# Hybrid attention and expert block: attention heads issued in three steps, and a split first product

## The chip, the cores and the metric

One core of a Trainium2 chip runs one program. The metric is the device time of one execution in microseconds (us). Each kernel is run several times and the median counts. One further execution is taken with the profiler on, and all rows below come from that one.

## What is computed

The reference is one decoder layer on 256 tokens of width 2048, in float32:

```
h   = RMSNorm(x)
z   = h @ w_in          # q, k, v of the window attention; q, kv, rope key of the latent attention; two gates
y_a = window attention, 16 heads of 64, 4 key heads, sinks and ALiBi   @ w_a_proj
y_b = latent attention, 8 heads of 128 + 64 rope, values of 128        @ w_b_proj
x   = x + (sigmoid(g_a) * y_a + sigmoid(g_b) * y_b) @ w_o
x   = x + PEER(RMSNorm(x))      # 8 heads, 16 of 16384 experts each
out = RMSNorm(x)
```

## The kernel before

**Numbers and weights.** Every float32 weight or activation is kept as a high part that TensorE reads at full rate and a low part, the remainder. `feed_hi` (L100) loads one megabyte of weights, 16 tiles of 128 x 128, into a ring of three buffers (SP's queue), ScalarE (ACT) makes the high part `whi` (L108) and VectorE (DVE) the low part `wlo` (L112), both in rings of two. `tblock` (L142) is one projection block of 128 output columns: for each of `nk` depth blocks a matmul of the high weight with the activation's high and low part side by side (L145, 512 columns), then for each one of the low weight with the activation's high part (L149, 256 columns). `tproj` (L343) is such a block over all 16 depth blocks, followed by `both` (L151: one copy on ACT, one addition on DVE) and a scaling (L346). `split` (L138) is the pair of an ACT copy and a DVE subtraction that makes an activation's two parts.

**Order.** Up to the expert part (`manual_schedule`, L920) the order of instructions on each engine is made by the framework's planner: it steps through an estimated time line and gives each engine the earliest program line whose operands it believes ready by then. Each engine works its list in order. Program order is thus a priority, and an engine waits when the real operands are later than the planner thought.

**Around the change.** The queries' eight blocks (`qT`, L448) come first. Then `gates(sga)` (L566) makes 16 blocks for the first gate, and after each one `work.pull(2.2)` (L569) lets the generator `swa` (L482) go on. `Work.pull` (L54) keeps an account: the budget is added, each yielded cost is taken off, and the generator runs while the account is positive. `swa` yields 2.0 after each head and 0.4 after each pair of heads. One head: four logit matmuls (`lg`, L498 and L499); softmax on DVE and ACT in `row_max`, `exps` (L452) and the first lines of `probs_T` (L460); three transposes of the normalised row `lt` (`tp`, L467); a split into `pT` (L513); six products with the values (`ot`, in `pv`, L476). Two heads share an `ot`, whose split (L516) fills one of the eight parts of `ya`.

`branch` (L573) then makes 16 blocks of half depth from `ya` and the first gate, with `work.pull(0.9)` for the latent heads' generator `mla` (L519): ten logit matmuls a head, and the operands of a head (`qns`, `kns`, `qrs`, `vs`) split in `prepare`, called for head h + 1 behind head h's products. `gates(sgb)` runs 16 blocks for the second gate, with the rest of `mla` beside them.

Later, the attention's output projection (L617) ends with a chain per block: `both`, the residual (L621), the gain (L631) and the split into `xc` (L632). The first of the 16 blocks of the expert queries (`tblock(ps, KO, xc)`, L781) needs all 16 parts of this `xc`, the last made last. Its transposes `x1t` (L611) are those of the residual rows. Behind it stands a matmul with ones (L786) for the norm.

Of the kernel before, what the change touches and what calls it, by code (L numbers as in the profile page):

```python
# [8 lines left out]
F32 = mybir.dt.float32  # L9
# [56 lines left out]
def block(tc, a, out):  # L66
# [72 lines left out]
        act.activation(hi, src, AF.Copy)  # L139
        vec.tensor_tensor(lo, src, hi.bitcast(F32), op=OP.subtract)  # L140

    def tblock(ps, nk, act_c, between=None):  # L142
        ws = take(nk)
        for k, (wh, wl) in enumerate(ws):
            pe.matmul(ps, wh, act_c[:, k].rearrange("p a t -> p (a t)"), start=k == 0, stop=False)  # L145
        if between:
            between()
        for k, (wh, wl) in enumerate(ws):
            pe.matmul(ps[:, :T], wl, act_c[:, k, 0], start=False, stop=k == nk - 1)  # L149

    def both(pl, ps):  # L151
        t = pl.tile([P, T], F32, name="both", bufs=2)
# [190 lines left out]
    def tproj(dst, scale=1.0):  # L343
        ps = acc_tile()
        tblock(ps, KO, xc)
        vec.scalar_tensor_tensor(dst, both(x0p, ps), scale, r1, op0=OP.mult, op1=OP.mult)  # L346
# [98 lines left out]
    for h in range(NH_B):  # L445
        uproj(knT[:, h], 2, ckvT)
    tmpp.close()
    for b in range(8):  # L448
        tproj(qT[:, b], 0.125)


    def exps(lt, m):  # L452
        nm = wk.tile([P, 2], F32, name="nm")
# [3 lines left out]
        act.activation(lt[:, 128:384], lt[:, 128:384], AF.Exp, bias=nm[:, 1:2], accum_out=ssm[:, 1:2])  # L457
        return nm, ssm

    def probs_T(lt, ssm):  # L460
        rec = wk.tile([P, 2], F32, name="rec")
        vec.reciprocal(rec, ssm)
        vec.tensor_scalar(lt[:, 0:128], lt[:, 0:128], rec[:, 0:1], None, op0=OP.mult)
        vec.tensor_scalar(lt[:, 128:384], lt[:, 128:384], rec[:, 1:2], None, op0=OP.mult)
        tp = tp_tile()
        for k in range(3):
            pe.transpose(tp[:, k * P:(k + 1) * P], lt[:, k * P:(k + 1) * P], ident)  # L467
        return tp

    def row_max(lt):  # L470
        m = wk.tile([P, 2], F32, name="mx")
# [4 lines left out]
    def pv(ot, vh, vl, pT, first, last):  # L476
        for c, o, ks in ((0, slice(0, 256), slice(0, 256)), (1, slice(128, 256), slice(256, 384))):
            pe.matmul(ot[:, o], vh[:, c], pT[:, 0, ks], start=first and c == 0, stop=False)
            pe.matmul(ot[:, o], vh[:, c], pT[:, 1, ks], start=False, stop=False)
            pe.matmul(ot[:, o], vl[:, c], pT[:, 0, ks], start=False, stop=last and c == 1)  # L480

    def swa(yc):  # L482
        def prepare(b):
            qs = wk.tile([P, 2, T], F32R, name="qs", bufs=1)
            stacked(qs, qT[:, b])
            return qs

        qs = prepare(0)
        for b in range(8):
            kp, i = b // 4, b % 4  # L490
            ot = ps_att.tile([P, 512], F32, name="ot", bufs=1)
            for half in range(2):
                g = 2 * kp + half
                h = g * 4 + i
                lg = ps_att.tile([P, 512], F32, name="lg", bufs=1)
                for q, ks, o in ((slice(0, 128), slice(0, 128), slice(0, 128)),
                                 (slice(128, 256), slice(0, 256), slice(128, 384))):
                    pe.matmul(lg[:, o], qs[:, half, q], kk[:, g, ks], start=True, stop=False)  # L498
                    pe.matmul(lg[:, o], qs[:, half, q], kl[:, g, ks], start=False, stop=True)  # L499
                if half and b < 7:  # L500
                    qs = prepare(b + 1)
                lt = wk.tile([P, 384], F32, name="lt", bufs=2)
                vec.scalar_tensor_tensor(lt, dist, -(2.0 ** (-8.0 * (h + 1) / NH_A)), lg[:, 0:384],
                                         op0=OP.mult, op1=OP.add)
                m = row_max(lt)
                vec.tensor_scalar(m, m, sink[:, h:h + 1], None, op0=OP.max)
                nm, ssm = exps(lt, m)
                e = wk.tile([P, 2], F32, name="esink")
                act.activation(e, nm, AF.Exp, bias=sink[:, h:h + 1])
                vec.tensor_tensor(ssm, ssm, e, op=OP.add)  # L510
                tp = probs_T(lt, ssm)
                pT = wk.tile([P, 2, 384], F32R, name="pTs", bufs=1)
                split(pT[:, 0], pT[:, 1], tp[:, 0:384])  # L513
                pv(ot, vap[:, 0, :, g], vap[:, 1, :, g], pT, half == 0, half == 1)
                yield 2.0
            split(yc[:, b, 0], yc[:, b, 1], ot[:, 0:256])  # L516
            yield 0.4

    def mla(yc):  # L519
        scale = 192.0 ** -0.5  # L520

        def prepare(h):
            if h % 2 == 0:
                qr[:] = [mw.tile([P, 2, T], F32R, name="qrs")]
                stacked(qr[0], qrT[:, h // 2])
            qn, kn = (mw.tile([P, 2, T], F32R, name=n) for n in ("qns", "kns"))
            split(qn[:, 0], qn[:, 1], qnT[:, h])
            split(kn[:, 0], kn[:, 1], knT[:, h])
            vs = mw.tile([P, 2, 2, P], F32R, name="vs")
            split(vs[:, 0], vs[:, 1], vb[:, :, h * P:(h + 1) * P])  # L530
            return qr[0], qn, kn, vs

        qr = []
        ops = prepare(0)
        for h in range(NH_B):
            half = h % 2
            qrs, qn, kn, vs = ops
            lg = ps_att.tile([P, 512], F32, name="lg", bufs=1)
            for q, ks, o in ((slice(0, 128), slice(0, 128), slice(0, 128)),
                             (slice(128, 256), slice(0, 256), slice(128, 384))):  # L540
                pe.matmul(lg[:, o], qn[:, 0, q], kn[:, 0, ks], start=True, stop=False)
                pe.matmul(lg[:, o], qn[:, 0, q], kn[:, 1, ks], start=False, stop=False)
                pe.matmul(lg[:, o], qn[:, 1, q], kn[:, 0, ks], start=False, stop=False)
                pe.matmul(lg[:, o], qrs[:, half, q], krT[:, 0, ks], start=False, stop=False)
                pe.matmul(lg[:, o], qrs[:, half, q], krT[:, 1, ks], start=False, stop=True)
            lt = wk.tile([P, 384], F32, name="lt", bufs=2)
            vec.scalar_tensor_tensor(lt, lg[:, 0:384], scale, cmask, op0=OP.mult, op1=OP.add)
            m = row_max(lt)
            nm, ssm = exps(lt, m)
            tp = probs_T(lt, ssm)  # L550
            pT = wk.tile([P, 2, 384], F32R, name="pTs", bufs=1)
            split(pT[:, 0], pT[:, 1], tp[:, 0:384])
            ot = ps_att.tile([P, 512], F32, name="ot", bufs=1)
            pv(ot, vs[:, 0], vs[:, 1], pT, True, True)
            if h + 1 < NH_B:
                ops = prepare(h + 1)
            yield 2.0
            split(yc[:, h, 0], yc[:, h, 1], ot[:, 0:256])
            yield 0.4

# [3 lines left out]
    def gates(sg):  # L566
        for b in range(KO):
            tproj(sg[:, b])
            work.pull(2.2)  # L569
        for q in range(4):  # L570
            act.activation(sg[:, 4 * q:4 * q + 4], sg[:, 4 * q:4 * q + 4], AF.Sigmoid)

# [5 lines left out]
    ya = yp.tile([P, 8, 2, T], F32R, name="ya", tag="y0")  # L578
    sga = yp.tile([P, KO, T], F32, name="sga")
    work.add(swa(ya))  # L580
    gates(sga)
    work.drain()
    swp.close()
# [3 lines left out]
    work.add(mla(yb))  # L587
    for b in range(KO):
        branch(ya, sga, x0p, b)
        work.pull(0.9)  # L590
    sgb = yp.tile([P, KO, T], F32, name="sgb", tag="y0")
    gates(sgb)
    work.drain()
# [184 lines left out]
    behind = None  # L778
    for hp in range(16):
        ps = acc_tile()  # L780
        tblock(ps, KO, xc)  # L781
        if hp:
            work.pull(1.2)
        if hp == 0:
# [399 lines left out]
```

## Time and profile before

| what | us |
|---|---|
| median of 3 runs | 1921.58 (1920.23 to 1923.5) |
| profiled execution, its own time | 1917.56 |
| span of that execution | 1915.8 |
| mean granted clock of TensorE over the span | 0.994 |
| queries' blocks, from the first one to the first logits | 108.1 to 158.1 |
| first gate's blocks with the window attention | 158.1 to 271.7 |
| branch blocks and second gate's blocks with the latent attention | 271.7 to 433.3 |
| first block of the expert queries, start to its norm's matmul | 572.0 to 581.2 |

In the trace an engine's line is its busy time; for TensorE, PE is matmuls and PEld the weight loads that run beside them. Matmuls are pipelined: a row's duration is longer than the distance to the next row's start, so prices of matmuls are read from starts. "idle before" in brackets is the time for which the engine stood before that instruction, and the instruction that ended it. The granted clock is given in parts of full speed, 1.0 for 2.4 GHz and 0.5 for 1.2 GHz, averaged over a stretch.

### The profile page before, as it was taken

The numbers are of one execution on the slowest core, as the hardware profiler recorded it, in microseconds if no ns is written. First come the engines' busy times: TensorE is split into PE (matmuls) and PEld (weight loads), VectorE is DVE, ScalarE is ACT, GpSimd is POOL, SyncE is SP. The second block draws the span as 40 slices with busy tenths as digits, with TensorE's granted clock in tenths as the row PEclk, the third lists the DMA queues.
The fourth block names the chain that finished last, engine by engine and source line by source line (L and its number), as shares of the span: only waits on it lengthen the run. The fifth ranks groups of instructions, "written<-read, shape, count | busy, mean of one in ns | idle before, by whom it ended". The sixth has DMA issues, their size and how long they took to land.

```text
span 1915.8 us, 28101 instructions
## 1 busy us (share of the span) xinstructions
PE 1871.1 (98%) x10874; PEld 1678.5 (88%) x10874; DVE 1594.7 (83%) x2277; ACT 1142.5 (60%) x1756; POOL 360.1 (19%) x192
## 2 busy tenths in 40 slices
PE   8999999999999999999999999999999999999996
PEld 6888888888888899999999999988888888887885
DVE  5767879658778889989799999899888888878887
ACT  7645666545555554555899999864444444444444
POOL 0000000000000000516243433333322222233210
PEclk9999999999999999999999999999999999999998
DMA  7554434455555566666889888879999999999983
GB/s 285 187 189 154 141 123 153 147 184 189 202 198 181 176 206 234 220 238 241 309 337 352 345 339 344 343 303 373 366 394 373 382 386 380 378 397 378 393 337 127
DMA packets 77910, 526.16 MB, mean 275 GB/s; under 512 B 9168, under 2 KB 11472, under 8 KB 15568
## 3 DMA queue, kind: packets, MB, share of 16 engines
q1 hardware_dynamic: 59344, 390.14, 56.4%
q0 software_dynamic: 18432, 134.23, 17.2%
q8 instruction: 85, 1.39, 0.3%
q14 instruction: 49, 0.40, 0.1%
HBM read 520.14 MB, written 4.19 MB: 274 GB/s over the span
## 4 chain that ended last, share of the span: by engine, by line
PE 64%; issue 13%; DVE 8%; POOL 7%; DMA 4%; ACT 4%; SPq 0%; POOLq 0%; DVEq 0%; ACTq 0%
PE acc L145 15%; PE o L1008 11%; PE acc L149 8%; POOL urow L803 7%; PE acc L927 6%; PE o L1025 5%; PE o L1026 5%; PE o L1027 5%; PE acc L956 4%; DVE wlo L112 3%; DMA raw<-v 3%; ACT whi L108 2%; PE acc L165 1%; PE acc L166 1%; PE acc L164 1%
## 5 line engine op out<-in xcount | busy, mean ns | idle before, releaser
L112 DVE TENSOR_TENSOR wlo<-raw,whi 128x2048 fp32r<-128x2048 f32 (+2 forms) x363 | 827.1, 2279 | 215.9 <-ACT whi L108 203.5
L108 ACT ACTIVATE whi<-raw 128x2048 fp32r<-128x2048 f32 (+2 forms) x363 | 688.6, 1897 | 435.1 <-DMA raw<-v 179.7
L927 PE MATMUL acc<-hc,whi 128*128 128x384 f32 x2048 | 383.0, 339 | 0.2 <-ACT whi L108 0.2
L927 PEld LDWEIGHTS acc<-hc,whi 128*128 128x128 f32 x2048 | 353.2, 189 | 0.4 <-ACT whi L108 0.4
L956 PE MATMUL acc<-hc,wlo 128*128 128x192 f32 x2048 | 251.2, 274 | 4.9 <-DVE wlo L112 4.9
L1008 PE MATMUL o<-wlo,wc 128*128 128x512 f32 x1020 | 252.2, 389 | 1.0 <-DVE wlo L112 1.0
L956 PEld LDWEIGHTS acc<-hc,wlo 128*128 128x128 f32 x2048 | 243.4, 192 | 6.0 <-DVE wlo L112 5.9
L145 PE MATMUL acc<-xc,whi 128*128 128x512 f32 x928 | 231.1, 395 | 1.5 <-DVE xc L140 1.5
L1008 PEld LDWEIGHTS o<-wlo,wc 128*128 128x128 f32 x1020 | 191.3, 188 | 41.4 <-DVE wlo L112 1.7
L803 POOL DMA_INDIRECT urow<-u_rows,iv x64 | 167.1, 2611 | 314.0 <-DVE urow L827 311.0
L1025 PE MATMUL o<-whi,wc 128*128 128x512 f32 x504 | 196.6, 390 | 3.6 <-ACT whi L108 1.8
L145 PEld LDWEIGHTS acc<-xc,whi 128*128 128x128 f32 x928 | 168.4, 188 | 32.5 <-DVE xc L140 1.7
L1026 PE MATMUL o<-whi,wc 128*128 128x512 f32 x504 | 196.1, 389 | 0.0
L1027 PE MATMUL o<-whi,wc 128*128 128x512 f32 x504 | 196.1, 389 | 0.0
L803 POOL DMA_INDIRECT vrow<-v_rows,iv x64 | 126.2, 1972 | 333.2 <-DVE h_nat L840 299.4
L827 DVE SCALAR_TENSOR_TENSOR urow<-urow,h_nat 128x2048 f32<-128x2048 f32 x64 | 146.2, 2284 | 21.4 <-DMA urow<-u_rows,iv 21.3
L696 POOL TENSOR_TENSOR cand<-tv 128x256 f32<-128x256 f32 x16 | 14.0, 891 | 739.4 <-DVE tv L689 642.4
L840 DVE SCALAR_TENSOR_TENSOR h_nat<-vrow,gg,h_nat 128x2048 f32<-128x2048 f32 x63 | 147.8, 2346 | 0.0
L877 ACT ACTIVATE ge<-acc 128x192 f32<-128x192 f32 x128 | 41.3, 323 | 151.5 <-PE acc L956 146.7
L149 PE MATMUL acc<-xc,wlo 128*128 128x256 f32 x928 | 126.1, 286 | 0.0
L149 PEld LDWEIGHTS acc<-xc,wlo 128*128 128x128 f32 x928 | 121.4, 193 | 4.3
L1025 PEld LDWEIGHTS o<-whi,wc 128*128 128x128 f32 x504 | 94.6, 188 | 24.7 <-ACT whi L108 3.1
(329 smaller groups left out, 2255.1 us busy)
## 6 DMA issues: line engine op xcount, KB each, us to landing
raw<-u SPq DMA_DIRECT2D x128, 1024.0 KB, 5.0
raw<-v SPq DMA_DIRECT2D x128, 1024.0 KB, 8.7
raw<-w_ga SPq DMA_DIRECT2D x16, 1024.0 KB, 4.9
raw<-w_gb SPq DMA_DIRECT2D x16, 1024.0 KB, 5.0
raw<-w_o SPq DMA_DIRECT2D x16, 1024.0 KB, 5.0
raw<-w_pq SPq DMA_DIRECT2D x16, 1024.0 KB, 5.0
raw<-w_q SPq DMA_DIRECT2D x8, 1024.0 KB, 4.9
raw<-w_a SPq DMA_DIRECT2D x8, 1024.0 KB, 4.8
```

The costliest lines, as they stand in the source:

```text
L108: act.activation(hi, raw, AF.Copy)
L112: vec.tensor_tensor(lo, raw, hi.bitcast(F32), op=OP.subtract)
L145: pe.matmul(ps, wh, act_c[:, k].rearrange("p a t -> p (a t)"), start=k == 0, stop=False)
L149: pe.matmul(ps[:, :T], wl, act_c[:, k, 0], start=False, stop=k == nk - 1)
L803: pool.indirect_dma_start(out=dst, out_offset=None, in_=table, in_offset=bass.IndirectOffsetOnAxis(ap=idx, axis=0))
L840: later(vec.scalar_tensor_tensor(h_nat, r, gg[:, i:i + 1], h_nat, op0=OP.mult, op1=OP.add))
L927: pe.matmul(ps[:, :2 * TD], wh, hc[:, k].rearrange("p a t -> p (a t)"), start=k == 0, stop=False)
L956: pe.matmul(ps[:, :TD], wl, hc[:, k, 0], start=False, stop=k == KO - 1)
L1008: pe.matmul(O[c][i], st_, v[:, i * 512:(i + 1) * 512], start=first and k == 0, stop=last and k == len(ss) - 1)
L1025: pe.matmul(O[0][i], S[0], vh[:, d], start=n == 0, stop=False)
L1026: pe.matmul(O[0][i], S[1], vh[:, d], start=False, stop=False)
L1027: pe.matmul(O[1][i], S[2], vh[:, d], start=n == 0, stop=False)
```

## The change

Three things are changed. `tblock` can put the last `late` depth blocks behind the others, high and low parts of the first ones first; the first block of the expert queries uses this with two. `probs_T` loses the normalisation (now `normalised`) and gains the split into `pT`. A new generator, `staged`, runs the heads in steps: each step does the products (`back`) of the head two before, the transposes and their split (`probs_T`) of the head before, and the operands, logits and softmax (`front`) of its own head, and yields 2.0. `swa` and `mla` are written as `front` and `back`. The generator of the window attention is now started before the queries' blocks, which pull 1.7 each from the second on; `gates` pulls 1.7 in place of 2.2, the branch blocks 0.8 in place of 0.9.

```diff
@@ -139,14 +139,16 @@
         act.activation(hi, src, AF.Copy)
         vec.tensor_tensor(lo, src, hi.bitcast(F32), op=OP.subtract)
 
-    def tblock(ps, nk, act_c, between=None):
+    def tblock(ps, nk, act_c, between=None, late=0):
         ws = take(nk)
-        for k, (wh, wl) in enumerate(ws):
-            pe.matmul(ps, wh, act_c[:, k].rearrange("p a t -> p (a t)"), start=k == 0, stop=False)
-        if between:
-            between()
-        for k, (wh, wl) in enumerate(ws):
-            pe.matmul(ps[:, :T], wl, act_c[:, k, 0], start=False, stop=k == nk - 1)
+        for ks in (range(nk - late), range(nk - late, nk)):
+            for k in ks:
+                pe.matmul(ps, ws[k][0], act_c[:, k].rearrange("p a t -> p (a t)"), start=k == 0, stop=False)
+            if between:
+                between()
+                between = None
+            for k in ks:
+                pe.matmul(ps[:, :T], ws[k][1], act_c[:, k, 0], start=False, stop=k == nk - 1)
 
     def both(pl, ps):
         t = pl.tile([P, T], F32, name="both", bufs=2)
@@ -445,9 +447,6 @@
     for h in range(NH_B):
         uproj(knT[:, h], 2, ckvT)
     tmpp.close()
-    for b in range(8):
-        tproj(qT[:, b], 0.125)
-
 
     def exps(lt, m):
         nm = wk.tile([P, 2], F32, name="nm")
@@ -457,15 +456,19 @@
         act.activation(lt[:, 128:384], lt[:, 128:384], AF.Exp, bias=nm[:, 1:2], accum_out=ssm[:, 1:2])
         return nm, ssm
 
-    def probs_T(lt, ssm):
+    def normalised(lt, ssm):
         rec = wk.tile([P, 2], F32, name="rec")
         vec.reciprocal(rec, ssm)
         vec.tensor_scalar(lt[:, 0:128], lt[:, 0:128], rec[:, 0:1], None, op0=OP.mult)
         vec.tensor_scalar(lt[:, 128:384], lt[:, 128:384], rec[:, 1:2], None, op0=OP.mult)
+
+    def probs_T(lt):
         tp = tp_tile()
         for k in range(3):
             pe.transpose(tp[:, k * P:(k + 1) * P], lt[:, k * P:(k + 1) * P], ident)
-        return tp
+        pT = wk.tile([P, 2, 384], F32R, name="pTs", bufs=1)
+        split(pT[:, 0], pT[:, 1], tp[:, 0:384])
+        return pT
 
     def row_max(lt):
         m = wk.tile([P, 2], F32, name="mx")
@@ -479,62 +482,79 @@
             pe.matmul(ot[:, o], vh[:, c], pT[:, 1, ks], start=False, stop=False)
             pe.matmul(ot[:, o], vl[:, c], pT[:, 0, ks], start=False, stop=last and c == 1)
 
+
+
+    def staged(n, front, back):
+        lts, pTs = [], []
+        for h in range(n + 2):
+            if pTs:
+                back(h - 2, pTs.pop(0))
+            if lts:
+                pTs.append(probs_T(lts.pop(0)))
+            if h < n:
+                lts.append(front(h))
+            yield 2.0
+
     def swa(yc):
         def prepare(b):
             qs = wk.tile([P, 2, T], F32R, name="qs", bufs=1)
             stacked(qs, qT[:, b])
             return qs
 
-        qs = prepare(0)
-        for b in range(8):
-            kp, i = b // 4, b % 4
-            ot = ps_att.tile([P, 512], F32, name="ot", bufs=1)
-            for half in range(2):
-                g = 2 * kp + half
-                h = g * 4 + i
-                lg = ps_att.tile([P, 512], F32, name="lg", bufs=1)
-                for q, ks, o in ((slice(0, 128), slice(0, 128), slice(0, 128)),
-                                 (slice(128, 256), slice(0, 256), slice(128, 384))):
-                    pe.matmul(lg[:, o], qs[:, half, q], kk[:, g, ks], start=True, stop=False)
-                    pe.matmul(lg[:, o], qs[:, half, q], kl[:, g, ks], start=False, stop=True)
-                if half and b < 7:
-                    qs = prepare(b + 1)
-                lt = wk.tile([P, 384], F32, name="lt", bufs=2)
-                vec.scalar_tensor_tensor(lt, dist, -(2.0 ** (-8.0 * (h + 1) / NH_A)), lg[:, 0:384],
-                                         op0=OP.mult, op1=OP.add)
-                m = row_max(lt)
-                vec.tensor_scalar(m, m, sink[:, h:h + 1], None, op0=OP.max)
-                nm, ssm = exps(lt, m)
-                e = wk.tile([P, 2], F32, name="esink")
-                act.activation(e, nm, AF.Exp, bias=sink[:, h:h + 1])
-                vec.tensor_tensor(ssm, ssm, e, op=OP.add)
-                tp = probs_T(lt, ssm)
-                pT = wk.tile([P, 2, 384], F32R, name="pTs", bufs=1)
-                split(pT[:, 0], pT[:, 1], tp[:, 0:384])
-                pv(ot, vap[:, 0, :, g], vap[:, 1, :, g], pT, half == 0, half == 1)
-                yield 2.0
-            split(yc[:, b, 0], yc[:, b, 1], ot[:, 0:256])
-            yield 0.4
+        cur, ots = [], []
+
+        def place(n):
+            b, half = n // 2, n % 2
+            g = 2 * (b // 4) + half
+            return b, half, g, g * 4 + b % 4
+
+        def front(n):
+            b, half, g, h = place(n)
+            if n == 0:
+                cur.append(prepare(0))
+            qs = cur[0]
+            lg = ps_att.tile([P, 512], F32, name="lg", bufs=1)
+            for q, ks, o in ((slice(0, 128), slice(0, 128), slice(0, 128)),
+                             (slice(128, 256), slice(0, 256), slice(128, 384))):
+                pe.matmul(lg[:, o], qs[:, half, q], kk[:, g, ks], start=True, stop=False)
+                pe.matmul(lg[:, o], qs[:, half, q], kl[:, g, ks], start=False, stop=True)
+            if half and b < 7:
+                cur[0] = prepare(b + 1)
+            lt = wk.tile([P, 384], F32, name="lt", bufs=2)
+            vec.scalar_tensor_tensor(lt, dist, -(2.0 ** (-8.0 * (h + 1) / NH_A)), lg[:, 0:384],
+                                     op0=OP.mult, op1=OP.add)
+            m = row_max(lt)
+            vec.tensor_scalar(m, m, sink[:, h:h + 1], None, op0=OP.max)
+            nm, ssm = exps(lt, m)
+            e = wk.tile([P, 2], F32, name="esink")
+            act.activation(e, nm, AF.Exp, bias=sink[:, h:h + 1])
+            vec.tensor_tensor(ssm, ssm, e, op=OP.add)
+            normalised(lt, ssm)
+            return lt
+
+        def back(n, pT):
+            b, half, g, h = place(n)
+            if not half:
+                ots[:] = [ps_att.tile([P, 512], F32, name="ot", bufs=1)]
+            pv(ots[0], vap[:, 0, :, g], vap[:, 1, :, g], pT, half == 0, half == 1)
+            if half:
+                split(yc[:, b, 0], yc[:, b, 1], ots[0][:, 0:256])
+
+        yield from staged(NH_A, front, back)
 
     def mla(yc):
         scale = 192.0 ** -0.5
-
-        def prepare(h):
-            if h % 2 == 0:
+        qr, vs = [], []
+
+        def front(h):
+            half = h % 2
+            if not half:
                 qr[:] = [mw.tile([P, 2, T], F32R, name="qrs")]
                 stacked(qr[0], qrT[:, h // 2])
+            qrs = qr[0]
             qn, kn = (mw.tile([P, 2, T], F32R, name=n) for n in ("qns", "kns"))
             split(qn[:, 0], qn[:, 1], qnT[:, h])
             split(kn[:, 0], kn[:, 1], knT[:, h])
-            vs = mw.tile([P, 2, 2, P], F32R, name="vs")
-            split(vs[:, 0], vs[:, 1], vb[:, :, h * P:(h + 1) * P])
-            return qr[0], qn, kn, vs
-
-        qr = []
-        ops = prepare(0)
-        for h in range(NH_B):
-            half = h % 2
-            qrs, qn, kn, vs = ops
             lg = ps_att.tile([P, 512], F32, name="lg", bufs=1)
             for q, ks, o in ((slice(0, 128), slice(0, 128), slice(0, 128)),
                              (slice(128, 256), slice(0, 256), slice(128, 384))):
@@ -547,16 +567,17 @@
             vec.scalar_tensor_tensor(lt, lg[:, 0:384], scale, cmask, op0=OP.mult, op1=OP.add)
             m = row_max(lt)
             nm, ssm = exps(lt, m)
-            tp = probs_T(lt, ssm)
-            pT = wk.tile([P, 2, 384], F32R, name="pTs", bufs=1)
-            split(pT[:, 0], pT[:, 1], tp[:, 0:384])
+            normalised(lt, ssm)
+            return lt
+
+        def back(h, pT):
+            vs = mw.tile([P, 2, 2, P], F32R, name="vs")
+            split(vs[:, 0], vs[:, 1], vb[:, :, h * P:(h + 1) * P])
             ot = ps_att.tile([P, 512], F32, name="ot", bufs=1)
             pv(ot, vs[:, 0], vs[:, 1], pT, True, True)
-            if h + 1 < NH_B:
-                ops = prepare(h + 1)
-            yield 2.0
             split(yc[:, h, 0], yc[:, h, 1], ot[:, 0:256])
-            yield 0.4
+
+        yield from staged(NH_B, front, back)
 
 
 
@@ -566,7 +587,7 @@
     def gates(sg):
         for b in range(KO):
             tproj(sg[:, b])
-            work.pull(2.2)
+            work.pull(1.7)
         for q in range(4):
             act.activation(sg[:, 4 * q:4 * q + 4], sg[:, 4 * q:4 * q + 4], AF.Sigmoid)
 
@@ -578,6 +599,10 @@
     ya = yp.tile([P, 8, 2, T], F32R, name="ya", tag="y0")
     sga = yp.tile([P, KO, T], F32, name="sga")
     work.add(swa(ya))
+    for b in range(8):
+        tproj(qT[:, b], 0.125)
+        if b:
+            work.pull(1.7)
     gates(sga)
     work.drain()
     swp.close()
@@ -587,7 +612,7 @@
     work.add(mla(yb))
     for b in range(KO):
         branch(ya, sga, x0p, b)
-        work.pull(0.9)
+        work.pull(0.8)
     sgb = yp.tile([P, KO, T], F32, name="sgb", tag="y0")
     gates(sgb)
     work.drain()
@@ -778,7 +803,7 @@
     behind = None
     for hp in range(16):
         ps = acc_tile()
-        tblock(ps, KO, xc)
+        tblock(ps, KO, xc, late=0 if hp else 2)
         if hp:
             work.pull(1.2)
         if hp == 0:
```

## Rows read from the trace of the kernel before

**Rows 1.** Engine totals of the span: busy us (share), instructions.

```profile
PE 1871.1 (98%) x10874; PEld 1678.5 (88%) x10874; DVE 1594.7 (83%) x2277; ACT 1142.5 (60%) x1756; POOL 360.1 (19%) x192
```

**Rows 2.** Stretches: length, busy us (instructions) by engine, clock, DMA share, GB/s.

```profile
158.14:271.70 113.56, 111.20 (x682) 94.95 (x681) 92.93 (x221) 76.18 (x155) 0.00 (x0) 1.00 0.43 144
271.70:334.90 63.20, 60.30 (x371) 51.80 (x370) 53.98 (x120) 41.62 (x92) 0.00 (x0) 1.00 0.39 130
```

**Rows 3.** Chain that ended last, undisturbed blocks: start us, us, what.

```profile
108.32 3.65 PE acc L145 x16
111.97 1.91 PE acc L149 x16
...
441.65 1.87 PE acc L145 x8
443.52 0.93 PE acc L149 x8
```

**Rows 4.** Timeline, TensorE: start us, us, engine, line, operation.

```profile
165.04 0.22 PE L498 MATMUL lg<-kk,qs 128*128 128x128 f32 x1
...
165.50 0.85 PE L145 MATMUL acc<-xc,whi 128*128 128x512 f32 x3
...
168.10 0.49 PE L467 MATMUL tp<-ident,lt 128*128 128x128 f32 x3
168.34 1.41 PE L145 MATMUL acc<-xc,whi 128*128 128x512 f32 x5
```

**Rows 5.** Waits of weight loads, 158.14 to 271.7: total us, times, longest.

```profile
PEld tp L467 <- DVE lt L463: 3.8, 10, 0.7
PEld ot L478 <- ACT pTs L139: 2.4, 7, 0.5
PEld tp L467 <- issue: 2.3, 4, 1.1
```

**Rows 6.** Waits of weight loads, 271.7 to 365.

```profile
PEld tp L467 <- DVE lt L463: 5.1, 8, 1.4
PEld ot L478 <- ACT pTs L139: 1.7, 4, 0.6
PEld ot L479 <- DVE pTs L140: 1.4, 3, 0.9
PEld acc L145 <- DVE ya L140: 1.1, 1, 1.1
PEld lg L542 <- DVE kns L140: 0.3, 1, 0.3
```

**Rows 7.** Timeline, first logits of heads 0 and 1, last scaling of heads 0 to 2.

```profile
158.25 0.22 PE L498 MATMUL lg<-kk,qs 128*128 128x128 f32 x1
...
161.65 0.33 PE L498 MATMUL lg<-kk,qs 128*128 128x128 f32 x1
...
166.40 0.35 DVE L464 TENSOR_SCALAR lt<-lt,rec 128x256 f32<-128x256 f32 x1
...
167.66 0.35 DVE L464 TENSOR_SCALAR lt<-lt,rec 128x256 f32<-128x256 f32 x1
...
177.54 0.35 DVE L464 TENSOR_SCALAR lt<-lt,rec 128x256 f32<-128x256 f32 x1
```

**Rows 8.** Timeline, first block of the expert queries.

```profile
572.01 3.66 PE L145 MATMUL acc<-xc,whi 128*128 128x512 f32 x15
...
577.21 0.43 DVE L140 TENSOR_TENSOR xc<-x1g,xc 128x256 fp32r<-128x256 f32 x1
...
577.69 0.50 PE L145 MATMUL acc<-xc,whi 128*128 128x512 f32 x1 [1.45 <-DVE xc L140]
578.02 3.40 PE L149 MATMUL acc<-xc,wlo 128*128 128x256 f32 x16
...
581.23 0.82 PE L786 MATMUL acc<-ssum,ones 128*128 128x256 f32 x2
```

**Rows 9.** Stretch around the clock's fall, columns as in rows 2.

```profile
575.00:580.00 5.00, 3.42 (x17) 2.68 (x17) 2.49 (x7) 3.10 (x4) 0.00 (x0) 0.83 0.88 306
```

## The prediction

> **What bounds the kernel now.** I read the engine totals first. TensorE's matmuls are busy 98% of the span [rows 1], so the kernel's length is TensorE's work plus what TensorE loses inside that "busy" time. Next the stretches. The two in which attention heads run beside projection blocks show PE busy 111.20 of 113.56 us and 60.30 of 63.20 us [rows 2]: by that row some 5 us are idle. A matmul's end is modelled, though, so I went on to start times. In the chain, where nothing disturbs it, a projection block is 3.65 + 1.91 = 5.56 us, or 0.228 us per 512-column matmul and 0.119 per 256-column one; a gate-times-branch block of half the depth is 1.87 + 0.93 = 2.80 us [rows 3]. A head adds four logit matmuls in 0.46 us (165.04 to 165.50) and three transposes in 0.24 us (168.10 to 168.34) [rows 4]; its six probability-times-value matmuls I estimate at the logits' 0.115 us each, 0.69 us. So a head costs 1.39 us of TensorE and one block plus one head 6.95 us.
>
> Third, the waits of the weight loads, which end TensorE's true stalls. First stretch: 3.8 us (10 times) before transposes whose normalised row is not there, 2.3 us more before transposes without a named releaser, 2.4 us before probability products whose split is late [rows 5]: 8.5 us. From 271.7 to 365 us: 5.1 us before transposes, 1.7 + 1.4 before probability products, 1.1 for the last part of ya, 0.3 for split keys: 9.6 us [rows 6]. Together 18.1 us that TensorE spends behind instructions its queue got too early; the ready matmuls stand behind them.
>
> **The change, part by part.** No matmul, transpose, activation or vector operation is added or dropped; attention issues no transfer, and POOL has no work in these stretches [rows 2]. What moves is the place in each engine's order. The planner puts an instruction where its own estimate says the operands are ready, earlier program lines first; the transposes of a head stood right behind its softmax and were put into the middle of the next block. Now a step holds the products of head h-2, the transposes of h-1 and the logits and softmax of h, and steps are one block apart (every 0.85 block at 1.7 against 2.0).
>
> (a) Probability products. Their split now has a whole step (6.95 us) between transposes and use, against the one ACT and one DVE instruction that the split is. Their waits go: 2.4 + 1.7 + 1.4 = 5.5 us [rows 5, 6]. Late next on TensorE is nothing of theirs, unless DVE falls a step behind.
>
> (b) ya. Its 18 steps start after the queries' second block; 1.7 per block over 23 blocks has them done after gate block 13 of 0 to 15, so the branch blocks find ya complete. 1.1 us goes [rows 6].
>
> (c) Transposes, the term with the widest bounds: none of 11.2 us (6.1 and 5.1), or all. What decides is the softmax chain against the step. From first logit to last scaled row the chain took 166.75 - 158.25 = 8.5 us for head 0, 168.01 - 161.65 = 6.4 for head 1, 177.89 - 165.04 = 12.9 for head 2 [rows 4, 7]; of the 16 sliding-window heads 4 stay under the 6.95 us step, of the 8 latent heads 5 stay under theirs, which is 2.5 branch blocks and one head, some 9.1 us. Nearest to the rows is therefore to let these shares go: 4/16 of 6.1 is 1.5 us and 5/8 of 5.1 is 3.2 us. 4.7 us go, 6.5 stay.
>
> (d) The latent heads' query and key splits. They move from behind the previous head's products into the step that uses them. One such wait cost 0.3 us [rows 6]; seven more at that price are 2.1 us lost. The bounds are nothing (the planner takes a split as soon as its buffer is free) and 6 us. The value split now sits just ahead of its products: its buffer has been free for a step, so I take nothing, within the same 6 us.
>
> (e) Order among other engines. The last sigmoids, the table loads that exponentials and sigmoids force on ACT, and the weight splits stay as many. ACT was busy 76.18 of 113.56 us, DVE 92.93 [rows 2]; spread over eight more blocks both get lighter. Weights are asked for in the same order on SP, one per block: no cost, and if that cover were gone it would show as waits for wlo.
>
> (f) The first block of the last product. Now 15 matmuls run from 572.01, the sixteenth waits for the last split row, ready at 577.21 + 0.43 = 577.64, and starts at 577.69; the 16 low matmuls then start at 578.02 and take until 581.23, 3.21 us where 1.91 is the undisturbed price, because the granted clock fell (mean 0.83 over 575 to 580, that is part of it at 1.2 instead of 2.4 GHz) right after TensorE had stood [rows 3, 8, 9]. With two blocks late, 14 high matmuls (3.19) and 14 low ones (1.67) end at 576.87, two transposes at about 577.1, the fifteenth goes, the sixteenth still starts at 577.69, and its low partners end near 578.2: 3.0 us earlier. The hole shrinks from about 2 us to some 0.4, so I take the clock as kept. If it falls anyway, 1.3 us of this is lost; if the row comes later, all of it could be. What is late next is the following block's weights, and that block needs none of the low ones for 3.65 us.
>
> **Sum.** 5.5 + 1.1 + 4.7 - 2.1 + 3.0 = 12.2 us. Behind 581 us TensorE is full to the end, so I carry it over whole. The profiled execution took 1917.56 us (span 1915.8); it becomes 1905.4. The median of the runs is 4.0 us higher, and from 1921.58 the forecast is **1909.4 us**. A difference under 0.2% (3.8 us) can't be told from none here.
>
> **The rivals.**
>
> *All transposes freed.* If the spread leaves DVE light enough that each chain fits its step, all 18.1 us and the 3.0 go, with no loss in (d): 21.1 us, 1900.5. For it: head 2, with the chain of 12.9 us, began at 165.04 while heads 0 and 1 were unfinished (166.75 and 168.01), and heads no longer overlap so. Against it: weight splits and block ends still stand between a chain's vector steps.
>
> *DVE binds the branch stretch.* From 271.70 to 334.90 DVE was busy 53.98 of 63.20 us, 85%, where weight loads were 82% [rows 2]; the change takes none of that work away and packs 0.4 head per branch block as before. If DVE's order sets the pace there, the waits of rows 6 come back as waits for wlo; left are 2.4 + 1.5 + 3.0 = 6.9 us: 1914.7. Against it: the last two heads' softmax of the first attention no longer falls into this stretch. A rule speaks for this rival: the Trainium skill, Perfetto Trace Analysis, Identifying the Most-Contended Engine, has occupancy as a fair measure for VectorE and says to improve the engine that has most of it. By that rule a reordering that leaves VectorE's work as it is gains nothing in this stretch; the trace agrees in so far as VectorE's row is ahead of the weight loads there.
>
> *It doesn't do what it says.* The planner had already chosen each place by its estimate, and may again set transposes and products to the moment it believes them ready. Then every wait stays, and only (f) is left: 1918.6, no change that can be told.
>
> *Slower: the softmax misses the step.* Products, transposes and next logits now stand together behind a block. If the planner keeps that order, a chain longer than the step holds TensorE at the transposes, with the new logits and the whole next block behind them. At head 0's 8.5 us that is 1.55 us for each of 16 sliding-window heads, 24.8 us, in place of the 8.5 of rows 5; with 3.0 from (f) that makes 1921.6 + 13.3 = 1934.9. It decides from a chain of 6.95 + 11.5/16 = 7.7 us. For it: three chains in four were longer. Against it: the planner did not keep such an order before, it put transposes between a block's matmuls.
>
> **How the numbers follow.** Forecast 0.52, all freed 0.08, DVE binds 0.18, does nothing 0.14, slower 0.08. The forecast's own band is 1904 to 1914 by the bounds of (c) and (d). The range takes that, DVE binding and "does nothing": 1902 to 1919, leaving out the slower case and most of the all-freed one. Faster by over 0.2% is the first three, 0.78; within 0.2% 0.14; slower 0.08.
>
> **What would show it.** Right: in the waits of the weight loads the probability products and ya are gone, transposes keep 5 to 8 us; no undisturbed run of blocks before the first logits at 158 us any more, the first ones near 119 us (108.3 and two blocks); the clock at 1.00 around 580 us, the last product's block with two matmul pairs behind the last split. (c) is wrong if transposes still cost 11 us; the whole forecast is wrong if waits for wlo in the branch stretch take what is freed, or if the transposes' wait grows above 1 us a head.

## The result, and the profile after

The changed kernel takes 1910.16 us (median of 7 runs, 1901.1 to 1913.53) against 1919.11 (1915.14 to 1923.5, 7 runs) for the kernel before: a ratio of 0.995, 95% interval 0.9932 to 0.9968 (estimated over all runs, not the quotient of the medians). In a later comparison it was 1907.75 (6 runs) against 1920.2 (10 runs), ratio 0.9932, interval 0.9911 to 0.9953. An eleventh run of the kernel before in that comparison took 10631.92 us and is left out as slow. The forecast was 1909.4 within 1902 to 1919, and faster.

The profiled execution after took 1913.5 us (span 1911.7), only 4.1 less than the one before. Distances between the starts of named matmuls show where that comes from. "First" is from the last up-projection matmul to the first branch matmul (ya), "second" from there to the first of yb, "product" from the last low matmul of the output projection to the norm's matmul. "Expert units" is from the first matmul of the expert units to the first of the values, "values" from there to the last matmul of the values. All are in us:

| | up to first | first | second | product | expert units | values | span |
|---|---|---|---|---|---|---|---|
| before | 108.0 | 163.7 | 161.4 | 9.5 | 638.8 | 586.3 | 1915.8 |
| after | 110.5 | 162.5 | 154.5 | 6.3 | 640.0 | 590.2 | 1911.7 |

The three changed places gain 1.2 + 6.8 + 3.2 = 11.2 us. The places that the change does not touch lost 2.5 before it and 1.2 + 3.9 behind it in this execution; what the table leaves out gained 0.4 in all. The repeats below show how far these places vary between executions.

The border between first and second cuts the work differently. The busy times of the kernel before (columns as in [rows 2]) show 970 and 932 matmuls in the two stretches:

```profile
108.04:271.73 163.69, 161.33 (x970) 139.25 (x969) 121.22 (x250) 99.05 (x176) 0.00 (x0) 1.00 0.46 155
271.73:433.09 161.36, 156.15 (x932) 135.87 (x930) 111.78 (x198) 89.23 (x148) 0.00 (x0) 1.00 0.45 154
```

The changed kernel has 979 and 923 (rows under "Four steps"): the last window head's three transposes and six products stood behind the first branch matmul and now stand ahead of it. At the prediction's 0.24 + 0.69 = 0.9 us for them, the gains like for like are some 2.1 us in the first stretch and 5.9 in the second, with the same sum.

The waits of the weight loads, first stretch and then second stretch of the changed kernel (total us, times, longest):

```profile
PEld tp L468 <- DVE lt L462: 6.5, 8, 1.2
PEld ot L481 <- issue: 0.3, 1, 0.3
...
PEld tp L468 <- DVE lt L462: 3.0, 4, 0.9
```

Against [rows 5] and [rows 6], the products with the values (`ot`) waited 2.4 + 3.1 us and now 0.3; ya's 1.1 us and the keys' 0.3 are gone. The transposes waited 6.1 and 5.1 us and now 6.5 and 3.0. In the first stretch they have lost nothing.

The timeline of TensorE for the first two heads shows why (start us, us, engine, line, operation):

```profile
128.26 3.59 PE L146 MATMUL acc<-xc,whi 128*128 128x512 f32 x15
132.47 0.33 PE L468 MATMUL tp<-ident,lt 128*128 128x128 f32 x1 [0.63 <-DVE lt L462]
132.56 0.48 PE L146 MATMUL acc<-xc,whi 128*128 128x512 f32 x1
132.88 0.38 PE L468 MATMUL tp<-ident,lt 128*128 128x128 f32 x2
...
139.20 0.33 PE L468 MATMUL tp<-ident,lt 128*128 128x128 f32 x1
...
140.75 2.06 PE L151 MATMUL acc<-xc,wlo 128*128 128x256 f32 x16
142.66 0.28 PE L481 MATMUL ot<-pTs,vap 128*128 128x256 f32 x1
```

The first head's transposes (L468, 132.47) are still in the middle of a block, between two of its matmuls, where the planner believed the row ready; the row is later and the block stands for it. The second head's products (L481, 142.66) come behind the rest of the block that its transposes (139.20) stand in, and find their operands.

The first head's row is late because its chain passes behind two weight splits in VectorE's list. Its first logits start at 121.78, and VectorE's timeline for it is:

```profile
122.43 2.29 DVE L112 TENSOR_TENSOR wlo<-raw,whi 128x2048 fp32r<-128x2048 f32 x1 [1.51 <-PE lg L520]
...
124.97 0.54 DVE L524 SCALAR_TENSOR_TENSOR lt<-dist,lg 128x384 f32<-128x384 f32 x1
...
128.41 2.29 DVE L112 TENSOR_TENSOR wlo<-raw,whi 128x2048 fp32r<-128x2048 f32 x1 [1.57 <-ACT whi L108]
...
131.09 0.15 DVE L531 TENSOR_TENSOR ssm<-ssm,esink 128x2 f32<-128x2 f32 x1
...
132.33 0.35 DVE L463 TENSOR_SCALAR lt<-lt,rec 128x256 f32<-128x256 f32 x1
```

One split (2.29 us) stands before the chain's first step, one in its middle; the chain takes 132.68 - 121.78 = 10.9 us.

The first block of the expert queries, answering to [rows 8]:

```profile
566.42 3.48 PE L146 MATMUL acc<-xc,whi 128*128 128x512 f32 x14
...
569.74 0.63 PE L151 MATMUL acc<-xc,wlo 128*128 128x256 f32 x4
...
570.49 1.43 PE L151 MATMUL acc<-xc,wlo 128*128 128x256 f32 x10
571.21 0.42 DVE L140 TENSOR_TENSOR xc<-x1g,xc 128x256 fp32r<-128x256 f32 x1
571.76 0.63 PE L146 MATMUL acc<-xc,whi 128*128 128x512 f32 x2
572.23 0.39 PE L151 MATMUL acc<-xc,wlo 128*128 128x256 f32 x2
572.45 0.59 PE L811 MATMUL acc<-ssum,ones 128*128 128x256 f32 x2
```

The last row still lands late (571.21 + 0.42, which is 5.5 us behind the start of the output projection's last low matmul; 5.9 before), but behind it are two pairs of matmuls (571.76 to 572.45) in place of one high and sixteen low ones.

### The profile page after: what moved, and what is told of

It reads as the page before. It is cut to its first block, busy times and chain, and to the rows that moved or that the text cites. A ratio compares the mean times of both kernels' runs of the same rounds, so it can differ in the third digit from the quotient of the medians.

```text
span 1911.7 us, 28123 instructions
## 1 busy us (share of the span) xinstructions
PE 1870.5 (98%) x10874; PEld 1680.9 (88%) x10874; DVE 1593.1 (83%) x2277; ACT 1139.8 (60%) x1754; POOL 349.9 (18%) x192
## 4 chain that ended last, share of the span: by engine, by line
PE 60%; issue 16%; POOL 8%; DVE 6%; DMA 5%; ACT 5%; SPq 0%; POOLq 0%; DVEq 0%; ACTq 0%
PE acc L146 15%; PE o L1033 8%; PE acc L952 8%; POOL urow L828 8%; PE acc L151 7%; PE acc L981 5%; PE o L1050 4%; DMA raw<-v 4%; PE o L1052 4%; PE o L1051 4%; DVE wlo L112 3%; ACT whi L108 3%; PE acc L167 1%; PE acc L168 1%; PE acc L166 1%
## 5 line engine op out<-in xcount | busy, mean ns | idle before, releaser
L828 POOL DMA_INDIRECT vrow<-v_rows,iv x64 | 116.1, 1814 | 347.3 <-DVE h_nat L865 317.3
L151 PE MATMUL acc<-xc,wlo 128*128 128x256 f32 x928 | 121.2, 283 | 0.0
```

Source lines behind the costliest of these rows:

```text
L151: pe.matmul(ps[:, :T], ws[k][1], act_c[:, k, 0], start=False, stop=k == nk - 1)
L828: pool.indirect_dma_start(out=dst, out_offset=None, in_=table, in_offset=bass.IndirectOffsetOnAxis(ap=idx, axis=0))
```

## The experiments

One theory stood against two rivals. **Places:** TensorE loses time behind instructions that its list holds before their operands are there; the change takes the products and ya out of that, and hardly the transposes. **Rivals:** VectorE's amount of work sets the pace; or the wider spacing of the heads, not their cutting, is what gains.

### Four steps

The transposes two steps behind their softmax, the products three:

```diff
-        for h in range(n + 2):
+        for h in range(n + 3):
             if pTs:
-                back(h - 2, pTs.pop(0))
-            if lts:
+                back(h - 3, pTs.pop(0))
+            if h >= 2 and lts:
                 pTs.append(probs_T(lts.pop(0)))
...
-            lt = wk.tile([P, 384], F32, name="lt", bufs=2)
+            lt = wk.tile([P, 384], F32, name="lt", bufs=3)
... # the same in the latent heads
-        junk = tp_.tile([P, 512], F32, name="njunk")
+        junk = tp_.tile([P, 512], F32, name="njunk", tag="qr")
```

> The transposes wait two steps behind their softmax and the products three; lt has three buffers, and a scratch row shares a buffer to make room. Places theory (TensorE loses time behind instructions that its list holds before their operands are there, and what is left of it in the changed kernel is 9.5 us at the transposes): the transposes' waits fall below 1.5 us; the first stretch (last up-projection matmul to first ya matmul, 162.5 us in the changed kernel) comes to 156 to 158, the second (first ya to first yb matmul, 154.5) to 151 to 153; the whole some 8 us below the changed kernel, 1899 to 1904. DVE theory (VectorE's amount of work sets the pace): the waits turn into waits for wlo, both stretches stay within 1 us of the changed kernel's.

Measured: 1896.02 us (4 runs), ratio to the kernel before 0.9898, interval 0.9852 to 0.9944. The total is 3 us below the stated 1899 to 1904; the runs side by side below put the step's own gain at 9.8 us. First stretch 156.5, second 151.3, both as the places theory had them. All that is left of the weight loads' waits in both stretches together is one row:

```profile
PEld lg L562 <- DVE kns L140: 0.2, 1, 0.2
```

The stretches' busy times, of the changed kernel first and of four steps below (columns as in [rows 2]):

```profile
110.54:273.06 162.52, 158.97 (x979) 140.78 (x978) 124.41 (x261) 99.93 (x184) 0.00 (x0) 1.00 0.45 153
273.06:427.58 154.52, 152.07 (x923) 135.17 (x922) 107.61 (x187) 85.59 (x138) 0.00 (x0) 1.00 0.49 164
```

```profile
107.58:264.11 156.53, 156.53 (x980) 141.18 (x979) 124.31 (x261) 99.33 (x183) 0.00 (x0) 1.00 0.47 162
264.11:415.44 151.33, 151.30 (x922) 134.91 (x921) 107.32 (x187) 85.71 (x138) 0.00 (x0) 1.00 0.49 165
```

VectorE did the same 124 and 107 us of work (over both stretches together 233.0 us in the kernel before, 232.0 in the changed one, 231.6 here); TensorE stands no more, and the stretches are 6.0 and 3.2 us shorter, about the 6.8 and 3.0 us that the weight loads had waited. The VectorE theory falls: its amount of work did not set the pace, the place of the transposes in TensorE's list against VectorE's order did. The third buffer of `lt` and the shared scratch row were not run by themselves, without the extra step; in the changed kernel no instruction of VectorE that writes `lt` waited. In TensorE's timeline of this kernel transposes now stand behind whole blocks, without a wait:

```profile
158.21 3.82 PE L146 MATMUL acc<-xc,whi 128*128 128x512 f32 x16
161.87 2.07 PE L151 MATMUL acc<-xc,wlo 128*128 128x256 f32 x16
...
164.41 0.51 PE L468 MATMUL tp<-ident,lt 128*128 128x128 f32 x3
164.68 0.31 PE L519 MATMUL lg<-kk,qs 128*128 128x128 f32 x1
```

### Staged without the early start

```diff
     for b in range(8):
         tproj(qT[:, b], 0.125)
-        if b:
-            work.pull(1.7)
...
-            work.pull(1.7)
+            work.pull(2.25)
```

> The changed kernel with its heads started only behind the queries' blocks, as before, with 2.25 pulled per gate block so that all 18 steps fit in 16 blocks. Places theory: products and ya no longer wait (under 1 us together in the first stretch), the transposes' waits in the first stretch are as large as before or larger (6 to 10 us) since steps are not further apart; first stretch 161 to 165, second as in the changed kernel, 153 to 156. Spread theory (the gain comes from the wider spacing): both gains vanish, first stretch 163 to 166 and second back at 159 or more.

Measured: 1909.2 us (one run), first stretch 164.3, second 155.4. First stretch's waits:

```profile
PEld tp L468 <- DVE lt L462: 6.2, 9, 0.9
PEld tp L468 <- issue: 0.6, 1, 0.6
PEld ot L482 <- DVE pTs L140: 0.5, 2, 0.3
...
PEld ot L481 <- ACT pTs L139: 0.4, 1, 0.4
```

The first stretch's 164.3 fits both theories; the second decides. Most of its gain is there without the early start, 6.0 of 6.8 us (0.9 of each is the last window head's work, which moved). In the first stretch next to nothing is gained on the 163.7 of before, 164.6 with that head. The early start with its smaller pull per gate block is worth 1.8 us in the first stretch and 0.9 in the second, beside the cutting. The pull is also that of the second gate's blocks, so this run can't tell the two apart.

### Spread without the steps

The uncut heads of the kernel before, started beside the queries' blocks, with the split first product:

```diff
-    for b in range(8):
-        tproj(qT[:, b], 0.125)
...
     work.add(swa(ya))
+    for b in range(8):
+        tproj(qT[:, b], 0.125)
+        if b:
+            work.pull(1.7)
...
-            work.pull(2.2)
+            work.pull(1.7)
```

> The heads of the kernel before, in one piece each, with the early start and the budget of 1.7 per block (latent heads 0.9 per branch block as before), and the split first product. Places theory: products still wait 3 to 5 us and transposes 9 to 12 over both stretches, only the wait for ya goes; first stretch 162.5 to 165 (it takes in the tail of the last head, 0.9 us), second 157 to 160. Spread theory (the wider spacing is what gains): first stretch under 161, second under 156.

Measured: 1920.6 us (one run), first stretch 166.5, second 159.0: the spread alone loses 2.8 us in the first stretch (I had bounded it at 165) and gains 2.4 in the second, together nothing. Of each, 0.9 is the last head's work that moved. Transposes wait 11.2 us in both stretches, as I had it; the products wait 7.9 us, more than my 3 to 5 and than the 5.5 before. The first stretch's largest waits:

```profile
PEld tp L466 <- DVE lt L462: 5.5, 12, 1.0
PEld ot L477 <- ACT pTs L139: 2.6, 8, 0.4
PEld ot L478 <- DVE pTs L140: 1.6, 5, 0.3
```

The spacing theory falls as well.

### Products one step later, transposes not

```diff
-        for h in range(n + 2):
+        for h in range(n + 1):
             if pTs:
-                back(h - 2, pTs.pop(0))
-            if lts:
-                pTs.append(probs_T(lts.pop(0)))
+                back(h - 1, pTs.pop(0))
             if h < n:
-                lts.append(front(h))
+                pTs.append(probs_T(front(h)))
```

> The changed kernel with the transposes back in the step of their own softmax and the products one step later. Places theory: the products' waits are gone (under 0.5 us), the transposes wait as in the changed kernel or up to 2 us more (9 to 12 us in both stretches); first stretch 162 to 164.5, second 154 to 157. If the step between softmax and transposes is what gained in the changed kernel, the second stretch is at 158 or more.

Measured: 1913.54 us (one run), first stretch 167.4, second 158.0. I missed this one. First stretch's waits, then the second's:

```profile
PEld tp L468 <- DVE lt L462: 6.6, 14, 1.0
PEld ot L481 <- ACT pTs L139: 2.8, 7, 0.8
PEld ot L482 <- DVE pTs L140: 0.9, 3, 0.4
...
PEld tp L468 <- DVE lt L462: 5.0, 7, 1.3
PEld ot L481 <- ACT pTs L139: 1.5, 4, 0.4
PEld ot L482 <- DVE pTs L140: 0.7, 2, 0.5
```

The products still wait, 6.2 us over both stretches. Counted in program lines they are a step behind the transposes; on TensorE the transposes have slid so far into the next block that the products stand right behind them again, two high matmuls and two low ones later in this part of the timeline:

```profile
189.19 0.70 PE L468 MATMUL tp<-ident,lt 128*128 128x128 f32 x3
189.65 0.71 PE L146 MATMUL acc<-xc,whi 128*128 128x512 f32 x2
190.19 0.40 PE L151 MATMUL acc<-xc,wlo 128*128 128x256 f32 x2
190.53 0.39 PE L481 MATMUL ot<-pTs,vap 128*128 128x256 f32 x1
```

With the second stretch at 158.0, the gain there needed the step between softmax and transposes, as the last sentence of the expectation had it. A step helps a consumer only if its producer does not slide into it: both edges, softmax to transposes and transposes to products, have to be longer than what the planner gets wrong.

The waits also account for the lengths of all six kernels so far. Taken off each stretch, they leave 155.7 to 156.5 us of the first (the kernel before 154.7, 155.6 with its last head) and 150.6 to 151.8 of the second, while the lengths themselves range from 156.5 to 167.4 and from 151.3 to 161.4. This run's first stretch is the longest because its waits, 11.5 us, are the largest.

### The split first product, alone and left out

```diff
 # the kernel before, with tblock's late
-        tblock(ps, KO, xc)
+        tblock(ps, KO, xc, late=0 if hp else 2)
```

> The kernel before with the split first product alone (two depth blocks late in the first block of the expert queries). Split theory: last output-projection matmul to the norm's matmul 6.3 us in place of 9.5, no fall of the clock there, both attention stretches as before (163.7 and 161.4). Rival (the clock falls because of what stood before, the heads' order): the clock still falls near 578 us and 8 us or more are left.

Measured: 1920.79 us (one run), product 6.25 us, no fall of the clock there, stretches 163.6 and 161.3. As expected, in its place; the total is within what one run tells.

```diff
 # the changed kernel
-        tblock(ps, KO, xc, late=0 if hp else 2)
+        tblock(ps, KO, xc, late=0)
```

> The changed kernel without the split first product. Split theory: last output-projection matmul to the norm's matmul back at 9 to 9.7 us with the clock falling in it, the stretches as in the changed kernel (162.5 and 154.5). Rival (the heads' order moved the clock's fall away): 8 us or less without a fall.

Measured: 1911.39 us (one run), product 8.27 us: the stand before the sixteenth matmul is back, but the clock did not fall. That is neither theory's number (9 to 9.7 with a fall, 8 or less without). So either the heads' order keeps the clock up, or the fall came by chance. Two more profiles, the kernel before and this one, unedited:

> The kernel before, profiled a second time. Sure-fall theory (the 2 us for which TensorE stands before the sixteenth block make the clock fall each time): last output-projection matmul to the norm's matmul 9.5 us again, with a fall at about 578. Chance theory (the same stand falls under a fall in some executions only): 8.3 us without one, as in the changed kernel without the split product. Stretches 163.7 and 161.4 within 0.3.

> The changed kernel without the split first product, profiled a second time. Sure-fall theory in the form that the heads' order took the fall away: 8.3 us again, no fall near 570. Chance theory: 8.3 without or 9.5 with a fall, either may come. Stretches 162.5 and 154.5 within 0.3.

Measured: the kernel before 1920.21 us with a product of 8.17 us and no fall near 580, stretches 163.7 and 161.3; the other 1910.23 us, 8.27, no fall, stretches 162.6 and 154.5. The kernel before, second profile:

```profile
578.79 0.44 PE L611 MATMUL x1t<-ident,x 128*128 128x128 f32 x2
580.68 0.50 PE L145 MATMUL acc<-xc,whi 128*128 128x512 f32 x1 [1.45 <-DVE xc L140]
581.02 2.07 PE L149 MATMUL acc<-xc,wlo 128*128 128x256 f32 x16
582.92 0.59 PE L786 MATMUL acc<-ssum,ones 128*128 128x256 f32 x2
```

The stand is the same 1.45 us as in [rows 8], the sixteen low matmuls take 582.92 - 581.02 = 1.90 us and not 3.21. The granted clock in the kernel before, first profile and then second (columns as in [rows 2]):

```profile
580.00:581.00 1.00, 1.00 (x6) 1.00 (x6) 0.00 (x0) 0.13 (x1) 0.00 (x0) 0.50 1.04 438
576.00:586.00 10.00, 8.47 (x45) 6.83 (x44) 7.30 (x12) 5.05 (x7) 0.00 (x0) 1.00 0.68 247
```

Of four profiles without the split one had the fall. The split was worth 1.9 to 2.0 us in the profiles without a fall (8.2 and 8.3 against 6.3) and 1.3 more against the one with it.

### The two versions side by side

The changed kernel and four steps, both as above, on one chip, five rounds.

> The changed kernel as it is, on the chip of the next run. Ratio to the kernel before 0.993 to 0.997; first stretch 162.5 us, second 154.5, first expert block 6.3, each within 0.3 us, whatever the total does: the rest of the spread comes from falls of the clock and from the value stage, outside the changed stretches.

> The version with four steps again, beside the changed kernel. Places theory: 9.2 us less than the changed kernel in the two stretches (156.5 and 151.3), so 0.4 to 0.5% less in the median, ratio to the kernel before 0.988 to 0.992. If the earlier total was luck of the clock, the median is within 4 us of the changed kernel's.

Measured: 1907.75 us (ratio 0.9932, 0.9911 to 0.9953) and 1897.99 us (0.9896, 0.9871 to 0.9922), so 9.8 us or 0.5% between their medians. Stretches 162.6 and 154.5 against 156.5 and 151.4, 9.3 us in all from unrounded starts. Four steps beat both kernels. The untouched places vary over the twelve profiles of this study: the time up to the first stretch from 106.3 to 111.1 us, the expert units from 634.6 to 642.0, the values from 585.6 to 592.2. The kernel before had 586.3 and 586.0 us for the values in its two profiles, the changed one 590.2 and 592.2, and the changed one without the split first product 588.4 and 588.5, so that a part may be the kernel's own; the medians, which fell by 9.0 and 12.4 us where the changed places gained 11.2, leave no room for a steady loss there of more than a few us. It was not followed up.

## Why the prediction was right

The total and its sign were right, by 12.2 us forecast against 11.2 in the changed places and 9.0 between the medians. That 1910.16 lies within 0.8 us of the forecast is luck: the forecast was counted from a median of 1921.58 (3 runs), and over 7 runs the kernel before came out 2.5 us lower. The mechanism held for `ya`, for the first block and, on a condition, for the products; the share of the transposes was mis-sized. Step by step:

(a) Products: 5.5 us forecast, 5.2 gone. The size is right; the reason held only because the transposes moved too, as the run with the products alone one step later shows.

(b) ya: 1.1 us forecast and gone.

(c) Transposes: the step that failed. "To let these shares go: 4/16 of 6.1 is 1.5 us and 5/8 of 5.1 is 3.2 us" took the chain's length against the step's. Measured went nothing in the first stretch (6.1 to 6.5) and 2.1 in the second (5.1 to 3.0), 1.7 of the 4.7 us. The step was also misread: 1.7 pulled against 2.0 is 0.85 step per block and not a step every 0.85 block, so steps come every 1.2 blocks, and first logits stand 8.0 us apart in the mean, not 6.95. Even so nothing went in the first stretch. The chains hardly got shorter as the heads drew apart (10.0 us in the mean of the 16 window heads before and 9.6 after, 8.3 and 8.5 for the latent heads), and the planner still set the transposes where it believed the row ready. What decides is whether the place is behind the real end of the chain; one more step does it, as four steps showed.

(d) Query and key splits: 2.1 us of loss forecast, none measured; no logits wait in the second stretch. The planner took these splits early: the first key split runs at 266.1, its logits at 275.9. So (c) was too large and (d) too pessimistic, 2.6 us net against about 2: two errors that nearly cancel, not two good estimates.

(e) Nothing forecast, and no wait for wlo appeared in either stretch.

(f) 3.0 us forecast, 3.2 measured between the two profiles. But the price held for an execution with a fall of the clock, which is one in four here; without a fall it is 1.9 to 2.0.

The carry-over is shown in the medians, not in the single profiles: with 5 to 7.5 us of spread in each of the stages outside the changed places, one pair of profiled executions differs by 4.1 us where 11.2 were gained.

Of the rivals, the "all transposes freed" case is what four steps reach, not three; the VectorE rival is not borne out here: with VectorE's work the same within 1.4 us, the two stretches together went from 325.1 to 317.0 and to 307.9 us. The prediction had the Trainium skill's rule on the most-contended engine (Perfetto Trace Analysis, Identifying the Most-Contended Engine) speak for this rival. The page says which engine to optimize first; that a new order gains nothing there was the prediction's own reading, and the runs show otherwise. "Does nothing" is true of the transposes in the first stretch alone. The slower case did not come: 12 waits at transposes of 0.8 us in the mean (6.5 + 3.0 us), not one of 1.55 at each head. The eight of the first stretch stood inside a block, as at 132.47, since the planner had moved them on from their step's place behind a block. The four of the second stood with the next head's logits, near their step's place, and cost 0.6 to 0.9 us each.

## What to carry to other kernels

These rules come from one kernel and six orders of it. Where a planner sets each engine's order by estimate, look for instructions that stand inside another group's run and wait there by a few tenths of a microsecond to about one each: the profile's PE row counts much of that time as busy, the weight loads' waits show it. Moving such an instruction later in program order helps only when it moves behind the real end of its operands' chain, and each edge of the chain has to be given that room: cutting at one edge let the next consumer stand again. Judge a gain of half a per cent by the distances between named matmuls, which repeat within 0.2 us, and by medians of several runs for the rest.

## What was not expected of the hardware

Behind the same stand of TensorE the clock falls in some executions and not in others. Before the sixteenth matmul of the first expert block TensorE stood 1.45 us in all four profiles without the split; one had a fall to 1.2 GHz (0.50) 0.6 us behind the stand's end and 1.3 us more of low matmuls, three had none (1.00). The other stand, 2.1 us ahead of the short key blocks (start at 104.53 in the kernel before), is the same in all twelve profiles; in five of them a fall to 0.50 comes within 0.7 us of its end. The time up to the first stretch is 109.6 to 111.1 us in these five and 106.3 to 108.6 in the other seven. The five are the first profile of the changed kernel, the second of the kernel before, the split first product alone, the steps without the early start and the spread without the steps, so this fall is no part of the change.
